# A fused hybrid encoder step: first norms run ahead, first operands built without GpSimd, and x re-read over tiles that are read early

## The chip, the cores and the metric

The kernel runs on 1 core of one Trainium2 chip. The metric is the device time of one execution in microseconds (us), of which the median over several runs is compared. The core has five engines with a queue of instructions each: TensorE (PE; its weight loads are PEld), VectorE (DVE), ScalarE (ACT), GpSimd (POOL) and SyncE (SP), which here issues the DMAs.

## The reference, cut to what matters

```python
mod = silu(c) @ w_ada + b_ada              # shift, scale, gate for 3 sub-layers
h = rms_norm(x) * gain * (1 + sc1) + sh1   # sub-layer 1
gate, up = split(h @ w_up);  x = x + 0.5 * g1 * ((silu(gate) * up) @ w_down)
h = adaRMS(x);  projections, stick-breaking heads, retention heads;  x = x + g2 * mixed
h = adaRMS(x);  x = x + 0.5 * g3 * swiglu(h)  # sub-layer 3
```

There are 1024 tokens of a new stream and 64 of a running one (1088 columns), D_MODEL = 1024 (8 tiles of 128 rows), D_FF = 2816 (22 tiles). All is fp32. The kernel splits each fp32 operand into a high and a low part, and makes each product of two operands from three matmuls (high x high, low x high, high x low).

## The kernel before, in words

x lies transposed in eight tiles `A0` to `A7` of 128 x 1088. The kernel runs in this order: a head (norm of sub-layer 1, its shift and scale, its operands), the up product of sub-layer 1 for f = 0 to 21, the down product of sub-layer 1, the mixed heads, sub-layer 3. The change touches the head, and by its placing of tiles the seam between the up and the down product.

**The head.** x comes in three chunks of columns (384, 384, 320). For each, ACT squares the eight tiles (L262), POOL and DVE add the squares up (`sq`, L265), PE folds them over partitions (`st`, L272), DVE and POOL make the row factors (`ra` L214, `rx` L215), PE spreads them over the partitions (`rb`, L221), and DVE multiplies x in place (L667 before, L669 after). The shift and scale of each of the eight tiles kt, in the order 0, 4, 1, 5, 2, 6, 3, 7, take the weight tiles `au`, PE sums (`pa`, L675), a copy to SBUF on DVE (`pe`), PE's turn of it (`pm`, L686), and on DVE `mod` and `scale_a`. `pa` and `pm` have one PSUM bank each.

**The first operands.** The up product is done with seven products instead of eight (a Strassen-Winograd scheme, `ORDER` p1, p6, p5, p7, p2, p4, p3). For each k = 0 to 3, from `A[k]` and `A[k+4]`, ACT makes four modulated blocks b11, b12, b21, b22 (L407, in tiles `hn`, eight buffers in all), DVE and POOL make four differences t1 = b12 - b11, t2 = b22 - t1, t3 = b22 - b12, t4 = b21 - t2 (L412), and each of seven of these is split: ACT casts the high part (L225), DVE or POOL subtracts it (L226). The matmuls of p1, p6 and p5 for f = 0 are taken k by k as the operands come; they read b11, t2 and t1. In the rows, `xt23` is the split of t2 for k = 3, `hn0t23` that difference before its split, and `xb` and `hn0b` the same for the b blocks.

**The weights.** `wr` are raw weight tiles (four buffers), `wh` and `wl` their high (ACT, L81) and low parts (POOL, L86), seven buffers each. `wr1s` and some `wr1a` are sums of raw tiles that DVE makes (L466).

**The seam.** The operands of the up product lie in 28 tiles, among them the eight A tiles. After f = 21 the kernel loads x into the A tiles again (L772 before, L779 after), for which the last product that reads a tile must be done. The down product then adds PE's result into A (`resid`, L243, on DVE). Beside it DVE makes the next modulation from the rows `wa` and the silu of c, `csil` (L743 before, L750 after), one step after the sixth of each eight results; here DVE goes in the order in which the program is written. PE writes its results to eight PSUM banks in turn. The SP queue starts each DMA in its place in the queue, after all that the DMA has to wait for.

Of the kernel before, what the change touches and what calls it, by code (L numbers as in the profile page):

```python
# [24 lines left out]
CHUNKS = [(0, 384), (384, 384), (768, 320)]  # L25
# [13 lines left out]
def drain(gen):  # L39
    for _ in gen:  # L40
        pass
# [74 lines left out]
def tile_hybrid_step(ctx: ExitStack, tc: tile.TileContext, I, O):  # L116
    nc = tc.nc
# [39 lines left out]
    def pt(tag, name):  # L157
        return psum.tile([P, 512], F32, tag=tag, name=name, bufs=BANKS[tag])
# [65 lines left out]
    def split_h(src, hi, lo, eng):  # L224
        nc.scalar.copy(hi, src)  # L225
        eng.tensor_tensor(lo, src, hi.bitcast(F32), op=ALU.subtract)  # L226
# [127 lines left out]
    SETS = ("b11", "t1", "t2", "b21", "t3", "t4", "b22")  # L354
# [27 lines left out]
    def x_whole(pool):  # L382

        tags = [(hpool, f"{t}{k}") for k in range(KT) for t in "HL"] + [(pool, f"xe{i + 2}") for i in range(4)]
        for k in range(4):
            for i, name in enumerate(SETS):
                if i < 5:
                    p, tag = tags[5 * k + i]
                else:
                    p, tag = xpool, f"A{k + 4 * (i - 5)}"  # L390
                yield k, name, p, tag

    def x_parts(parts, pool, n, k, s, whole):

        w = 2 * BL if whole else BL
        b = {}

        def new(name):
            return pool.tile([P, w], F32, tag="hn", name=f"hn{n}{name}{k}{s}", bufs=8)

        for name, kt, lo, x in parts:
            h = b[name] = new(name)
            if not whole:
                nc.vector.tensor_tensor(h, A[kt][:, lo:lo + w], x, op=ALU.mult)
            src = A[kt][:, lo:lo + w] if whole else h
            for s0, sw, bt in ([(lo, w, 0)] if lo + w <= NPR else [(lo, NPR - lo, 0), (NPR, NSM, 1)]):
                nc.scalar.activation(h[:, s0 - lo:s0 - lo + sw], src[:, s0 - lo:s0 - lo + sw], AF.Identity,  # L407
                                     bias=mod[:, 3 * n, bt, kt:kt + 1], scale=scale_a[:, n, bt, kt:kt + 1])

        def less(name, x, y, eng):  # L410
            t = b[name] = new(name)
            eng.tensor_tensor(t, b[x], b[y], op=ALU.subtract)  # L412

        less("t1", "b12", "b11", nc.vector)
        less("t2", "b22", "t1", nc.vector)
        less("t3", "b22", "b12", nc.gpsimd)
        less("t4", "b21", "t2", nc.vector)
        return b

    def x_build_whole(k, n, pool, places):  # L420

        h = 2 * BL
        b = x_parts((("b11", k, 0, None), ("b12", k, h, None), ("b21", k + 4, 0, None), ("b22", k + 4, h, None)),
                    pool, n, k, "", True)
        for i, name in enumerate(("b11", "t2", "t1", "t3", "b21", "t4", "b22")):
            p, tag = places[k, name]
            t = p.tile([P, NTOK], F32R, tag=tag, name=f"x{name}{k}", bufs=1)
            split_h(b[name], t[:, :h], t[:, h:], nc.gpsimd if i in (1, 3, 5) else nc.vector)
            for part in range(2):
                for s in range(2):  # L430
                    X[name, part, k, s] = t[:, (2 * part + s) * BL:(2 * part + s + 1) * BL]
# [190 lines left out]

    xe = tc.alloc_tile_pool(name="xe1", bufs=1, reuse_waits="tile")
    places = {(k, name): (p, tag) for k, name, p, tag in x_whole(xe)}
    up = Up(1, I["wup1"], hd[:FFT])
    with tc.tile_pool(name="st", bufs=1, reuse_waits="tile") as pool:
        pools["tmp"] = pool
        cT = pool.tile([P, KT, 2], F32, name="cT")
        bada = pool.tile([P, 9, KT], F32, name="bada")
        for t, nm in ((cT, "cT"), (bada, "bada"), (gains, "gains")):  # L630
            nc.sync.dma_start(t, I[nm])
        adau, adae = {}, {}
        pairs = [0, 4, 1, 5, 2, 6, 3, 7]

        def ada_load(kt):
            for s in (1, 0):
                t = adau[s, kt] = pool.tile([P, D], F32, tag="au", name=f"au{s}_{kt}", bufs=4)
                nc.sync.dma_start(t, I["wada01"][s * KT + kt])

        for c, (c0, w) in enumerate(CHUNKS):  # L640
            for k in range(KT):
                nc.sync.dma_start(A[k][:, c0:c0 + w], I["x"][k][:, c0:c0 + w])
        for kt in pairs[:2]:
            ada_load(kt)
        weights = up.prep(0)
        next(weights)
        next(weights)
        cS = pool.tile([P, KT, 32], F32, name="cS")
        nc.gpsimd.memset(cS, 0.0)
        nc.scalar.activation(cS[:, :, 0:2], cT, AF.Silu)  # L650
        sel = pool.tile([P, 2], F32, name="sel")
        nc.vector.tensor_reduce(sel, ident.rearrange("p (j x) -> p x j", x=32)[:, 0:2, :],
                                axis=mybir.AxisListType.X, op=ALU.add)
        for kt in pairs[2:]:
            ada_load(kt)
        nc.sync.dma_start(qkg, I["qkg"])

        ns = [Norm(0, c, pool, ("pj", "z", "wt")[c]) for c in range(3)]

        def norm_first(c):  # L660

            c0, w = CHUNKS[c]
            ns[c].fold()
            ns[c].factors()
            ns[c].rows(("pj", "z", "wt")[c])
            for kt in pairs:
                nc.vector.tensor_tensor(A[kt][:, c0:c0 + w], A[kt][:, c0:c0 + w], ns[c].rb[:, :w], op=ALU.mult)  # L667

        def ada_sums(kt):  # L669

            pa = pt("ms", f"pa{kt}")
            for s in (1, 0):
                for k in range(KT):
                    j = k % 4
                    nc.tensor.matmul(pa[32 * j:32 * j + 32, s * P:(s + 1) * P], cS[:, k, :],  # L675
                                     adau[s, kt][:, k * P:(k + 1) * P], start=k < 4, stop=k >= 4)
            pe = adae[kt] = pool.tile([P, 256], F32, tag="pe", name=f"pe{kt}", bufs=2)
            with tc.high_priority(offset=500):
                nc.vector.tensor_copy(pe, pa[:, :256])

        def ada_turn(kt):

            pe = adae.pop(kt)
            pm = pt("av", f"pm{kt}")
            for s in (1, 0):
                nc.tensor.matmul(pm[:, 2 * s:2 * s + 2], pe[:, s * P:(s + 1) * P], sel, start=True, stop=True)  # L686
            with tc.high_priority(offset=500):
                for s in (1, 0):
                    nc.vector.tensor_scalar(mod[:, s, :, kt], pm[:, 2 * s:2 * s + 2], bada[:, s, kt:kt + 1], None,
                                            op0=ALU.add)  # L690
                nc.vector.tensor_scalar(scale_a[:, 0, :, kt], mod[:, 1, :, kt], 1.0, gains[:, 0, kt:kt + 1],
                                        op0=ALU.add, op1=ALU.mult)

        with tc.manual_schedule(engines={mybir.EngineType.PE}):
            for c in range(3):
                for d in range(KT):
                    ns[c].square(d)
                norm_first(c)
            ada_sums(pairs[0])
            ada_sums(pairs[1])  # L700
            drain(weights)
            for k in range(4):
                for kt in pairs[2 * k:2 * k + 2]:
                    ada_turn(kt)
                if k < 3:
                    for kt in pairs[2 * k + 2:2 * k + 4]:
                        ada_sums(kt)
                if k > 0:
                    for p in ORDER[:3]:
                        for s in range(2):  # L710
                            up.product(0, p, s, [k - 1])
                x_build_whole(k, 0, pool, places)
            for p in ORDER[:3]:
                for s in range(2):
                    up.product(0, p, s, [3])
# [610 lines left out]
    for i, blk in enumerate((0, 2, 1, 3)):  # L1326
        c0 = blk * BL
# [64 lines left out]
    for g in range(FFT // 2):  # L1392
        for _, final in down.steps(g):
            if final is not None:
                c, d = final
                c0, w = CHUNKS[c]
# [100 lines left out]
```

## Time and profile before

| | us |
|---|---|
| median of 3 runs | 2334.13 |
| lowest and highest | 2331.98 to 2338.8 |
| profiled execution, device time | 2335.12 |
| its span | 2333.3 |
| PE busy | 2192.5 (94%) |
| DVE busy | 1510.1 (65%) |
| POOL busy | 1078.1 (46%) |
| ACT busy | 833.6 (36%) |

The span runs from the first to the last instruction of the profiled execution. Its device time is 1.8 us longer, and stands 1.0 us above the median. Busy shares are means over the whole span.

### The profile page before, as it was taken

How to read it: one execution, taken by the hardware profiler on the slowest of the kernel's cores; microseconds unless marked ns; L12 is line 12 of the kernel's file. 1: busy time of each engine (PE TensorE's matmuls, PEld its weight loads, DVE VectorE, ACT ScalarE, POOL GpSimd, SP SyncE). 2: the span in 40 equal slices, each digit the busy share in tenths (PEclk: the TensorE clock that was granted, in tenths of full speed). 3: DMA queues.
4: the chain of work that ended last, by engine and by line, in shares of the span. 5: the costliest groups of instructions: out<-in, count | busy, mean ns of one | idle time of the engine just before them, and what ended most of it. 6: DMA issues, size and time to landing. Idle time of an engine off the chain costs nothing. (4 is left out here: it accounts for less than half of the span.)

```text
span 2333.3 us, 40156 instructions
## 1 busy us (share of the span) xinstructions
PE 2192.5 (94%) x15188; PEld 2147.3 (92%) x15188; DVE 1510.1 (65%) x2886; ACT 833.6 (36%) x1724; POOL 1078.1 (46%) x1020
## 2 busy tenths in 40 slices
PE   5799999998999988888989999967999999999999
PEld 4799999998999988888889998967999999999999
DVE  5867677654777777787784455477555555556666
ACT  4533232332122336665663333156322223322221
POOL 4644444453444556444343444255444444544442
PEclk9799999999999989999999999977999999999999
DMA  6233333336434311010101112122222222353323
GB/s 234 89 124 119 120 121 128 116 115 203 133 118 136 119 54 62 32 41 24 39 26 62 40 36 103 49 86 74 93 80 89 91 93 74 108 179 86 102 81 101
DMA packets 116609, 220.35 MB, mean 94 GB/s; under 512 B 14528, under 2 KB 55488, under 8 KB 116416
## 3 DMA queue, kind: packets, MB, share of 16 engines
q1 hardware_dynamic: 116416, 217.79, 28.4%
q8 instruction: 120, 1.97, 0.4%
q14 instruction: 73, 0.60, 0.1%
HBM read 174.88 MB, written 42.86 MB: 93 GB/s over the span
## 5 line engine op out<-in xcount | busy, mean ns | idle before, releaser
L243 DVE SCALAR_TENSOR_TENSOR A<-dn,mod,A 128x384 f32<-128x384 f32 (+1 forms) x704 | 329.8, 496 | 149.5 <-PE dn L199 148.9
L197 PE MATMUL dn<-hs,wh 128*128 128x384 f32 (+1 forms) x1056 | 348.8, 330 | 7.9 <-DVE A L243 7.9
L198 PE MATMUL dn<-hs,wl 128*128 128x384 f32 (+1 forms) x1056 | 348.0, 330 | 0.0
L199 PE MATMUL dn<-hl,wh 128*128 128x384 f32 (+1 forms) x1056 | 348.0, 330 | 0.0
L86 POOL TENSOR_TENSOR wl<-wr,wh 128x512 fp32r<-128x512 f32 x162 | 220.6, 1368 | 136.2 <-ACT wh L81 131.3
L226 POOL TENSOR_TENSOR hl<-hr,hs 128x384 fp32r<-128x384 f32 x132 | 132.7, 1022 | 239.1 <-ACT hs L225 237.1
L197 PE MATMUL pj<-Hh,wh 128*128 128x384 f32 (+1 forms) x672 | 237.0, 353 | 2.3 <-DVE A L243 2.3
L199 PE MATMUL pj<-Lh,wh 128*128 128x384 f32 (+1 forms) x672 | 224.5, 334 | 0.0
L198 PE MATMUL pj<-Hh,wl 128*128 128x384 f32 (+1 forms) x672 | 223.1, 332 | 0.0
L197 PEld LDWEIGHTS dn<-hs,wh 128*128 128x128 f32 x1056 | 199.1, 189 | 8.3 <-DVE A L243 8.2
L198 PEld LDWEIGHTS dn<-hs,wl 128*128 128x128 f32 x1056 | 199.1, 189 | 0.0
L199 PEld LDWEIGHTS dn<-hl,wh 128*128 128x128 f32 x1056 | 199.0, 188 | 0.0
L518 DVE TENSOR_TENSOR u<-p,p 128x272 f32<-128x272 f32 x176 | 77.3, 440 | 167.7 <-PE p L199 167.7
L225 ACT CAST hs<-hr 128x384 fp32r<-128x384 f32 x132 | 65.3, 496 | 328.3 <-PE dn L198 154.9
L197 PE MATMUL p<-xt,wh1s 128*128 128x272 f32 x528 | 154.5, 293 | 2.5 <-DVE u L518 2.5
L198 PE MATMUL p<-xt,wl1s 128*128 128x272 f32 x528 | 154.2, 292 | 0.0
L199 PE MATMUL p<-xt,wh1s 128*128 128x272 f32 x528 | 153.9, 292 | 0.2
L81 ACT CAST wh<-wr 128x512 fp32r<-128x512 f32 x162 | 98.1, 619 | 148.7 <-PE wo L199 50.1
L86 POOL TENSOR_TENSOR wl1a<-wr1a,wh1a 128x512 fp32r<-128x512 f32 x66 | 93.3, 1415 | 94.6 <-ACT wh1a L81 88.2
L86 POOL TENSOR_TENSOR wl2a<-wr2a,wh2a 128x512 fp32r<-128x512 f32 x66 | 87.5, 1327 | 102.0 <-ACT wh2a L81 101.2
L197 PEld LDWEIGHTS pj<-Hh,wh 128*128 128x128 f32 x672 | 129.0, 192 | 5.3 <-issue 3.3
L198 PEld LDWEIGHTS pj<-Hh,wl 128*128 128x128 f32 x672 | 129.1, 192 | 0.3
(326 smaller groups left out, 6723.5 us busy)
## 6 DMA issues: line engine op xcount, KB each, us to landing
wa<-in_wada SPq DMA_DIRECT2D x56, 512.0 KB, 3.6
hd<-hh SPq DMA_DIRECT2D x44, 544.0 KB, 2.8
wr1a<-in_wup SPq DMA_DIRECT2D x88, 256.0 KB, 2.8
wr<-in_wdn SPq DMA_DIRECT2D x88, 256.0 KB, 2.9
wr2a<-in_wup SPq DMA_DIRECT2D x88, 256.0 KB, 2.8
hr<-hd SPq DMA_DIRECT2D x88, 192.0 KB, 2.7
wr<-in_win SPq DMA_DIRECT2D x56, 256.0 KB, 2.7
au<-in_wada SPq DMA_DIRECT2D x16, 512.0 KB, 4.7
```

The lines of the kernel that those rows point to most:

```text
L81: self.nc.scalar.copy(h, raw)
L86: self.nc.gpsimd.tensor_tensor(l, raw, h.bitcast(F32), op=ALU.subtract)
L197: nc.tensor.matmul(ps[:, :w], wh, xh, start=first, stop=False, skip_group_check=read_between)
L198: nc.tensor.matmul(ps[:, :w], wl, xh, start=False, stop=False, skip_group_check=read_between)
L199: nc.tensor.matmul(ps[:, :w], wh, xl, start=False, stop=last, skip_group_check=read_between)
L225: nc.scalar.copy(hi, src)
L226: eng.tensor_tensor(lo, src, hi.bitcast(F32), op=ALU.subtract)
L243: nc.vector.scalar_tensor_tensor(A[d][:, s0:s0 + sw], ps[:, s0 - c0:s0 - c0 + sw], mod[:, s, b, d:d + 1], A[d][:, s0:s0 + sw], op0=ALU.mul ...
L518: nc.vector.tensor_tensor(new(name), ps[:, :BL], v[y, s], op=ALU.add)
```

## The change

All row sums and factors of the three chunks are now written ahead of the products with them (the products of a chunk come after the next chunk's factors, those of the last chunk with the pair of tiles that needs them). The sums of a pair of tiles and their turns are written together, a pair earlier. t3 and the low parts that POOL had (16 instructions of 128 x 544 in all) are made on DVE. And in the placing of the 28 operand tiles the A tiles get t2 and t1, where they had t4 and b22.

```diff
@@ -383,7 +383,7 @@
         for k in range(4):
-            for i, name in enumerate(SETS):
+            for i, name in enumerate(("b11", "b21", "t3", "t4", "b22", "t2", "t1")):
                 if i < 5:
                     p, tag = tags[5 * k + i]
                 else:
@@ -413,7 +413,7 @@
-        less("t3", "b22", "b12", nc.gpsimd)
+        less("t3", "b22", "b12", nc.vector if whole else nc.gpsimd)
@@ -422,10 +422,10 @@
-        for i, name in enumerate(("b11", "t2", "t1", "t3", "b21", "t4", "b22")):
+        for name in ("b11", "t2", "t1", "t3", "b21", "t4", "b22"):
...
-            split_h(b[name], t[:, :h], t[:, h:], nc.gpsimd if i in (1, 3, 5) else nc.vector)
+            split_h(b[name], t[:, :h], t[:, h:], nc.vector)
@@ -658,12 +658,14 @@
         def norm_first(c):
-
-            c0, w = CHUNKS[c]
             ns[c].fold()
             ns[c].factors()
             ns[c].rows(("pj", "z", "wt")[c])
-            for kt in pairs:
+
+        def scaled(c, kts):
+
+            c0, w = CHUNKS[c]
+            for kt in kts:
                 nc.vector.tensor_tensor(A[kt][:, c0:c0 + w], A[kt][:, c0:c0 + w], ns[c].rb[:, :w], op=ALU.mult)
@@ -696,15 +698,20 @@
                 norm_first(c)
-            ada_sums(pairs[0])
-            ada_sums(pairs[1])
+                if c > 0:
+                    scaled(c - 1, pairs)
+            for kt in pairs[:2]:
+                ada_sums(kt)
+            for kt in pairs[:2]:
+                ada_turn(kt)
             drain(weights)
             for k in range(4):
-                for kt in pairs[2 * k:2 * k + 2]:
-                    ada_turn(kt)
+                scaled(2, pairs[2 * k:2 * k + 2])
                 if k < 3:
                     for kt in pairs[2 * k + 2:2 * k + 4]:
                         ada_sums(kt)
+                    for kt in pairs[2 * k + 2:2 * k + 4]:
+                        ada_turn(kt)
```

A scheduler orders what is written, except on PE in the head and on DVE beside the down product. Three places show what it made of it.

The first place is DVE in the head, from the factors of the first chunk on: `A0` to `A7` are the products with the row factors `rb0_0`, `sq0_1_4` is the sum of squares of the second chunk and `ra` the start of its factors. Before:

```order
L214 TENSOR_SCALAR ra_268<-st0_0_260 128x3
L265 TENSOR_TENSOR sq0_1_4_294<-sq0_1_4_294,sq0_1_5_296 128x384
L667 TENSOR_TENSOR A0_75<-A0_75,rb0_0_271 128x384
L667 TENSOR_TENSOR A4_79<-A4_79,rb0_0_271 128x384
L667 TENSOR_TENSOR A1_76<-A1_76,rb0_0_271 128x384
L667 TENSOR_TENSOR A5_80<-A5_80,rb0_0_271 128x384
L667 TENSOR_TENSOR A2_77<-A2_77,rb0_0_271 128x384
L667 TENSOR_TENSOR A6_81<-A6_81,rb0_0_271 128x384
L667 TENSOR_TENSOR A3_78<-A3_78,rb0_0_271 128x384
L667 TENSOR_TENSOR A7_82<-A7_82,rb0_0_271 128x384
L265 TENSOR_TENSOR sq0_1_4_294<-sq0_1_4_294,sq0_1_6_299 128x384
```

After it the same stretch reads:

```order
L214 TENSOR_SCALAR ra_268<-st0_0_260 128x3
L265 TENSOR_TENSOR sq0_1_4_286<-sq0_1_4_286,sq0_1_5_288 128x384
L669 TENSOR_TENSOR A0_75<-A0_75,rb0_0_271 128x384
L265 TENSOR_TENSOR sq0_1_4_286<-sq0_1_4_286,sq0_1_6_291 128x384
L669 TENSOR_TENSOR A4_79<-A4_79,rb0_0_271 128x384
L265 TENSOR_TENSOR sq0_1_4_286<-sq0_1_4_286,sq0_1_7_294 128x384
L669 TENSOR_TENSOR A1_76<-A1_76,rb0_0_271 128x384
L214 TENSOR_SCALAR ra_305<-st0_1_297 128x3
L669 TENSOR_TENSOR A5_80<-A5_80,rb0_0_271 128x384
```

The adds of the second chunk moved between the products of the first, and its factors ahead of five of them; the third chunk's stand in the same way among the second's products.

The second place is DVE at the last of the four blocks, k = 3, down to `u2`, the first step behind the head that reads PE's products. Before:

```order
L412 TENSOR_TENSOR hn0t13_794<-hn0b123_786,hn0b113_784 128x544
L412 TENSOR_TENSOR hn0t23_796<-hn0b223_791,hn0t13_794 128x544
L226 TENSOR_TENSOR xb113_802<-hn0b113_784,xb113_802 128x544
L412 TENSOR_TENSOR hn0t43_800<-hn0b213_789,hn0t23_796 128x544
L226 TENSOR_TENSOR xt13_808<-hn0t13_794,xt13_808 128x544
L226 TENSOR_TENSOR xb213_814<-hn0b213_789,xb213_814 128x544
L226 TENSOR_TENSOR xb223_820<-hn0b223_791,xb223_820 128x544
L466 TENSOR_TENSOR wr1a11_1_897<-wr1a11_1_897,wr1a21_1_895 128x512
L518 TENSOR_TENSOR u2_10_0_850<-p6_10_0_592,p1_10_0_846 128x272
```

And after:

```order
L412 TENSOR_TENSOR hn0t23_796<-hn0b223_791,hn0t13_794 128x544
L412 TENSOR_TENSOR hn0t33_798<-hn0b223_791,hn0b123_786 128x544
L412 TENSOR_TENSOR hn0t43_800<-hn0b213_789,hn0t23_796 128x544
L226 TENSOR_TENSOR xb113_802<-hn0b113_784,xb113_802 128x544
L226 TENSOR_TENSOR xt23_805<-hn0t23_796,xt23_805 128x544
L226 TENSOR_TENSOR xt13_808<-hn0t13_794,xt13_808 128x544
L226 TENSOR_TENSOR xt33_811<-hn0t33_798,xt33_811 128x544
L226 TENSOR_TENSOR xb213_814<-hn0b213_789,xb213_814 128x544
L226 TENSOR_TENSOR xt43_817<-hn0t43_800,xt43_817 128x544
L226 TENSOR_TENSOR xb223_820<-hn0b223_791,xb223_820 128x544
L466 TENSOR_TENSOR wr1a11_1_897<-wr1a11_1_897,wr1a21_1_895 128x512
L518 TENSOR_TENSOR u2_10_0_850<-p6_10_0_600,p1_10_0_846 128x272
```

t3 and the splits of t2, t3 and t4 joined DVE's row: eleven instructions of 128 x 544 for a k (with the first, t1, above the piece), where it had seven.

The third place is the SP queue at the seam: `wr2` to `wr5` are raw weights of the down product, `A1_0` to `A1_7` the tiles into which x is loaded, `hd21` takes the last result of the up product to memory. Before, x stood behind five weight tiles, and the rows of the modulation right behind x:

```order
L76 DMA wr2_0_6497<-in_wdn1 128x512
L76 DMA wr2_1_6499<-in_wdn1 128x512
L76 DMA wr3_0_6582<-in_wdn1 128x512
L76 DMA wr3_1_6584<-in_wdn1 128x512
L76 DMA wr4_0_6766<-in_wdn1 128x512
L772 DMA A1_0_6450<-in_x 128x384
L772 DMA A1_1_6451<-in_x 128x384
```

After, the 24 loads of x follow `wr2_0`, and this stands between the last of them and the modulation's rows:

```order
L779 DMA A1_7_6457<-in_x 128x320
L76 DMA wr2_1_6499<-in_wdn1 128x512
L76 DMA wr3_0_6582<-in_wdn1 128x512
L76 DMA wr3_1_6584<-in_wdn1 128x512
L76 DMA wr4_0_6766<-in_wdn1 128x512
L76 DMA wr4_1_6768<-in_wdn1 128x512
L542 DMA hd21_112<-hh121_6390 128x1088
L76 DMA wr5_0_6847<-in_wdn1 128x512
L733 DMA csil7_6485<-in_cond 128x1024 x2
L741 DMA wa7_0_6557<-in_wada 128x1024
```

The loads of x moved ahead of four weight tiles and of `hd21`, and seven transfers moved in between x and `csil`, `wa`. On ACT two casts of these weights now stand before and behind the last silu of the up product, `wh2_1` ahead of it. Beyond the head and the seam the rows of all engines are those of before.

## Rows read from the trace of the kernel before

**Rows 1.** The page's slices: PE busy in tenths, 40 slices of 58.3 us.

```profile
PE   5799999998999988888989999967999999999999
```

**Rows 2.** Windows: busy us (instructions) of PE, PEld, DVE, ACT, POOL; PE clock, DMA share, GB/s.

```profile
60.00:70.00 10.00, 7.61 (x90) 6.65 (x90) 9.67 (x14) 5.59 (x11) 8.30 (x5) 0.66 0.02 6
```

**Rows 3.** Waits of PE from 100 to 800 us: total, times, longest.

```profile
PE dn L197 <- DVE A L243: 7.9, 1, 7.9
```

**Rows 4.** Timeline of DVE in the head: start, duration, instruction [idle before, releaser].

```profile
17.18 3.81 DVE L667 TENSOR_TENSOR A<-A,rb 128x384 f32<-128x384 f32 x8 [2.46 <-PE rb L221]
20.90 2.50 DVE L265 TENSOR_TENSOR sq<-sq,sq 128x384 f32<-128x384 f32 x4
25.38 0.16 DVE L214 TENSOR_SCALAR ra<-st 128x3 f32<-128x3 f32 x1 [1.98 <-PE st L272]
...
28.42 3.80 DVE L667 TENSOR_TENSOR A<-A,rb 128x384 f32<-128x384 f32 x8 [2.46 <-PE rb L221]
32.14 0.21 DVE L214 TENSOR_SCALAR ra<-st 128x2 f32<-128x2 f32 x2
...
42.14 0.23 DVE L691 TENSOR_SCALAR scale_a<-mod,gains 128x2 f32<-128x2 f32 x1
```

**Rows 5.** Timeline of DVE: t1 of k = 0, 2, 3, a step alone, steps beside POOL.

```profile
44.11 0.71 DVE L412 TENSOR_TENSOR hn0t<-hn0b,hn0b 128x544 f32<-128x544 f32 x1
...
71.27 0.71 DVE L412 TENSOR_TENSOR hn0t<-hn0b,hn0b 128x544 f32<-128x544 f32 x1
...
74.70 0.71 DVE L412 TENSOR_TENSOR hn0t<-hn0b,hn0t 128x544 f32<-128x544 f32 x1
75.34 1.87 DVE L226 TENSOR_TENSOR xt<-hn0t,xt 128x544 fp32r<-128x544 f32 x1
77.13 3.64 DVE L226 TENSOR_TENSOR xb<-hn0b,xb 128x544 fp32r<-128x544 f32 x2
80.70 1.87 DVE L412 TENSOR_TENSOR hn0t<-hn0b,hn0b 128x544 f32<-128x544 f32 x1
...
91.82 0.78 DVE L518 TENSOR_TENSOR u<-p,p 128x272 f32<-128x272 f32 x2
```

**Rows 6.** Timeline of POOL in the same stretch.

```profile
74.90 5.29 POOL L226 TENSOR_TENSOR xt<-hn0t,xt 128x544 fp32r<-128x544 f32 x3 [1.41 <-ACT xt L225]
```

**Rows 7.** Timeline of ACT: the two parts of b22 for k = 0.

```profile
45.16 1.11 ACT L407 ACTIVATE hn0b<-A,mod,scale_a 128x480 f32<-128x480 f32 x2
```

**Rows 8.** Timeline of PE: the first matmul behind the head's products.

```profile
92.31 0.60 PE L197 MATMUL p<-xt,wh1s 128*128 128x272 f32 x1 [2.48 <-DVE u L518]
```

**Rows 9.** Timeline of the SP queue at the seam.

```profile
544.16 4.22 SPq L772 DMA_DIRECT2D A<-in_x  x9
...
550.18 8.47 SPq L772 DMA_DIRECT2D A<-in_x  x15
...
559.64 0.96 SPq L734 DMA_DIRECT2D wa<-in_wada  x2
```

**Rows 10.** Timeline of DVE at the seam.

```profile
532.46 0.44 DVE L518 TENSOR_TENSOR u<-p,p 128x272 f32<-128x272 f32 x1 [1.06 <-PE p L199]
...
568.31 1.23 DVE L743 SCALAR_TENSOR_TENSOR junk<-wa,csil 128x1024 bf16<-128x1024 f32 x1 [13.89 <-DMA wa<-in_wada]
```

**Rows 11.** Timeline of ACT at the seam: a cast behind p5, the silu behind p3.

```profile
535.45 0.62 ACT L81 CAST wh<-wr 128x512 fp32r<-128x512 f32 x1 [2.40 <-PE p L199]
...
548.02 0.43 ACT L539 ACTIVATE c<-c 128x272 f32<-128x272 f32 x1
```

**Rows 12.** Windows at the seam, columns as in rows 2.

```profile
565.00:570.00 5.00, 0.00 (x0) 0.00 (x0) 1.69 (x4) 2.11 (x2) 0.00 (x0) 0.66 0.85 335
```

**Rows 13.** Timeline of PE behind its wait at the seam.

```profile
570.13 0.69 PE L197 MATMUL dn<-hs,wh 128*128 128x384 f32 x1 [7.88 <-DVE A L243]
...
573.47 0.34 PE L198 MATMUL dn<-hs,wl 128*128 128x384 f32 x1
573.65 0.34 PE L199 MATMUL dn<-hl,wh 128*128 128x384 f32 x1
```

## The prediction

> **What bounds the kernel now.** I read the slices first: PE is at 9 tenths in most of them, and the first two stand at 5 and 7 [rows 1]. What is cheap to lose there is all that the head holds back from PE, so I looked for the places where PE waits. From 100 to 800 us there is one, 7.9 us long, on the DVE step that adds a result into A [rows 3]. The change touches the head and this seam; the rest of the program keeps its order on every engine, PE-bound, and will shift as a block. The reader is to see two different limits.
>
> In the head DVE is the limit: in the window from 60 to 70 us it is busy 9.67 of 10 us, and POOL 8.30 [rows 2]. It is busy, but much of it is waiting inside the instruction. A step of 128 x 544 alone is followed by the next after 0.64 us (74.70 to 75.34). The three steps from 75.34 run beside three POOL steps and take until 80.77, 5.43 us [rows 5, 6]. Alone they would take 1.9, so each POOL step costs DVE (5.43 - 1.9) / 3 = 1.18 us. PE goes on without breaks from 92.31, after DVE's first `u` at 91.82 [rows 5, 8].
>
> At the seam the wait's last link reads as DVE, but DVE itself stands 13.89 us for `wa` [rows 10]. It takes its steps in written order, so the results behind `wa` stay in their banks, and PE runs out of banks at 570.13 - 7.88 = 562.25. The row of `wa` is issued at 559.64, behind the 24 loads of x that begin at 544.16 [rows 9], and is in at 568.31. PE starts 1.82 us after that [rows 10, 13]. So the SP queue and the DMA engines, at 335 GB/s in that window [rows 12], set the end of this wait; the loaded x is not what comes last.
>
> **The change, part by part.**
>
> *Norms ahead of products.* The last add of the second chunk's squares on DVE stood third of four from 20.90 that took 2.50, so it ended near 22.8 [rows 4]. Now it stands behind two products and one add from 17.18, at 0.48 each (3.81 / 8), and ends near 19.1. From that add to `ra` are 2.55 us (22.8 to 25.38), from `ra` to the first product 3.04 (25.38 to 28.42) [rows 4]. I carry both over: `ra` of chunk 2 at 21.7, its products from 24.7, the third chunk's last add four products and two adds later and done by 26.7, its `ra` at 29.25 instead of 32.14. The sums and turns of the first pair hang on this, so `scale_a` at 42.14 [rows 4] comes 2.9 us earlier, near 39.3. The five products behind each `ra` cost nothing more, since they fill part of the 3.04 us in which PE and POOL make the factors; without that cover they cost 5 x 0.48 = 2.4. Ahead of the first t1 now stand two weight sums and three products, some 3.1 us, so t1 of k = 0 moves only from 44.11 [rows 5] to about 42.4: **-1.7**.
>
> *POOL's 16 steps on DVE.* Four a k: each adds 0.64 and takes away 1.18 of blocking. The bound on the good side is 16 x (1.18 - 0.64) = 8.6 us. The bound on the bad side is that nothing comes back and each costs 1.18 + 0.64 = 1.82 beside weight splits: 29 us more. I take the value cycle by cycle, since other waits appear once POOL is out. The blocks and differences have eight buffers, as many as one k uses, so b22 of the next k can be written only when the last split of this k is done. ACT needs 1.1 us for it [rows 7], then 0.55 for the cast behind it; DVE has one t1 (0.64) to do meanwhile. A clean k is then 11 x 0.64 + 1.0 = 8.0 us.
> - k = 0 and 1 took 71.27 - 44.11 = 27.2 us [rows 5]. After: 2 x 8.0, six weight splits of POOL, which stay (6 x 1.0, less than 1.18 as some fall into idle time), seven copies and turns with their two-engine round trips (about 5.0), one weight sum 0.6: 27.6, **+0.4**.
> - k = 2 took 80.70 - 71.27 = 9.4, after 8.0: **-1.4**.
> - k = 3 up to `u` took 91.82 - 80.70 = 11.1. After: 8.0 + one weight split 1.2 + one weight sum 0.6 = 9.8: **-1.3**.
>
> Together the head gives -4.0, and PE goes on near 88.3 instead of 92.31. Its clock there is no part of the sum: it starts from a half-idle stretch before and after. The Trainium skill, page "Perfetto Trace Analysis", section "Optimizing Scalar/DVE Operations", speaks against this part: when VectorE is saturated it says that handing work to ScalarE, or even GpSimd, may make sense, and this does the reverse; the same sentence adds that the two share a read port, so that the hand-over might not help. By its first half the 16 steps would lengthen a saturated engine by 16 x 0.64 = 10 us; by its second half and the 1.18 above they shorten it, and the sum goes by the row.
>
> *Turns pair by pair.* PE turns a pair before the products of the k before instead of behind them. This moves DVE's small steps earlier, inside the 27.6 above. What would be late is the first copy of the next sums, behind PE's products of 18 matmuls; the round trip has that in it. The load of `qkg` and two bias rows move behind the `au` loads; sub-layer 2 uses them hundreds of us later, so 21 passes of the up product hide them, and without that cover they would cost one landing.
>
> *The seam.* The loads of x wait for the last reader of each tile. A0 to A3 now hold t2, read by p6, whose second half was done by 532.46; A4 to A7 hold t1, read by p5, done by 535.45 [rows 10, 11]. Before they began at 544.16 [rows 9]. x is 128 x 1088 x 8 x 4 bytes = 4.46 MB. Five loads (0.98 MB) fit before 535.45; the other 3.47 MB need 10.4 us at 335 GB/s and end near 546. The weight tile `wr2_1` comes next and lands near 548.4. ACT's cast of it (0.62) now stands ahead of the last silu, which was at 548.02 [rows 11] and moves to 549. Behind that silu wait the last product with it on DVE, `hd21` on SP, and behind `hd21` one weight tile, `csil` and `wa`. So `wa` is issued near 553 instead of 559.64. From 550.5 on, two weight tiles, `hd21`, `csil` and `wa` are still to move: 0.52 + 0.56 + 1.05 + 0.52 = 2.65 MB, 7.9 us. `wa` is in near 558.4, ten us earlier. PE does not wait if it is in by 562.25 - 1.82 = 560.4. So the 7.88 goes, and its follow-up too: the granted clock of 565 to 570 is 0.66 [rows 12], PE has stood, and the ten matmuls from 570.13 take 3.34 us, at the lower of the two levels (1.2 of 2.4 GHz), against 10 x 0.18 at 573.47 [rows 13]: 1.5 us. **-9.4**. What is next in line is the tenth weight tile's slot, which needs POOL's split of `wr2_1`; that is about 550.5 and inside the sum.
>
> Sum: -4.0 - 9.4 = -13.4 us, from the profiled 2335.12 to 2321.7. The median of the runs is 1.0 us below the profiled time, so 2320.7; I say 2321.
>
> **The rivals.**
>
> *The head gives nothing (17%).* The two-engine round trips and the eight buffers leave DVE idle as long as POOL blocked it. For it: +0.4 in k = 0 and 1 already shows how little is left. Against: k = 2 and 3 have no turns in them. Time: 2334 - 9.4 = 2325.
>
> *The head gives all (10%).* The waits overlap, and the whole 8.6 and a head start of 2.9 come through: 2334 - 9.4 - 11.5 = 2313.
>
> *The wait at the seam stays (12%).* Seven more transfers, 2.1 MB, now stand between x and `wa`, and a late `wr2_1` holds ACT, DVE and `hd21` in turn. Each us by which `wr2_1` lands after 550.4 (548.4 plus the spare 2.0) is a us of PE's wait. With `wa` at 566 the wait is still 5.6 and the clock falls too: 2334 - 4.0 - 2.3 = 2328. For it: PE's row already blamed the wrong engine once. Against: x starts 11.7 us earlier (532.46 against 544.16), and 2.1 MB take 6.4.
>
> *DVE becomes the bound (6%), slower.* If POOL's steps are not what stretches DVE's, the 16 come on top at 1.23 us, the middle of 0.64 and 1.82: 19.7 us, against the start's 1.7 and the seam's 9.4: 2334 + 8.6 = 2343. It decides from (1.7 + 9.4) / 16 = 0.7 us net for a moved step. For it: DVE is at 9.67 of 10 us [rows 2]. Against: the step at 74.70 took 0.64 while POOL stood, and 1.87 right after beside it [rows 5, 6].
>
> **How the numbers follow.** The forecast has 55%, with its own range 2317 to 2326 (the head between -1 and -7, the seam between -7.5 and -9.4). The range 2313 to 2328 leaves out the slower case, half of the seam's rival and little of the one with all gains. A run of this kernel tells 0.3% (7.0 us) from no change. Faster by more than that: the forecast, the full gain, nearly all of the head's rival and a third of the seam's, 0.85. Within it: 0.09. Slower: 0.06.
>
> **What would show it.** In the head: steps of 128 x 544 on DVE at 0.64 to 0.72 except beside weight splits, `scale_a` of the first pair near 39.5, PE without breaks from about 88. At the seam: loads of x from about 532, `wa` issued near 553, no wait of PE on A, and no lower clock behind it. Wrong would be: DVE idle by many us for ACT's blocks or PE's turns in the head; a silu or `hd21` long behind 551; or a PE wait that moved to another step.

## The result and the profile after

| | before | after |
|---|---|---|
| median of the runs | 2334.13 us (2329.82 to 2338.8) | 2316.76 us (2316.09 to 2324.65) |
| profiled execution | 2335.12 us, span 2333.3 | 2316.76 us, span 2314.7 |
| ratio after / before | | 0.9938, 95% interval 0.992 to 0.9957 |

The change takes 17.4 us off the median and 18.6 us off the profiled span, against 13 forecast. The ratio over all runs says less, 14.5 us (10 to 18.7): three of the five runs after lie at 2316 to 2317 us, the other two at 2321.7 and 2324.7. Three rows of PE divide the 18.6, since each has the same matmul in both traces: the first behind `u` in the head [rows 8], the first behind the wait at the seam [rows 13], and, in the projection that follows, the first `pj` that waits for A (called the `pj` row below). After:

```profile
84.42 0.39 PE L197 MATMUL p<-xt,wh1s 128*128 128x272 f32 x1 [0.90 <-DVE u L518]
...
556.77 0.44 PE L197 MATMUL dn<-hs,wh 128*128 128x384 f32 x1 [3.40 <-DVE A L243]
...
825.56 0.41 PE L197 MATMUL pj<-Hh,wh 128*128 128x384 f32 x1 [1.71 <-DVE A L243]
```

The `pj` row of the kernel before, in the same view:

```profile
838.83 0.41 PE L197 MATMUL pj<-Hh,wh 128*128 128x384 f32 x1 [2.34 <-DVE A L243]
```

- **Head**: PE goes on at 84.42 instead of 92.31, -7.9 us. Forecast -4.0.
- **From there to the `pj` row**: 825.56 - 84.42 = 741.1 instead of 838.83 - 92.31 = 746.5, -5.4 us. Forecast -9.4 (the seam). PE runs dry at 556.77 - 3.40 = 553.37 where it was 562.25, so some 1.0 of the 5.4 came just behind the head, and 4.4 at the seam.
- **Rest**: 2314.7 - 825.56 = 1489.1 instead of 2333.3 - 838.83 = 1494.5, -5.3 us. Forecast nothing.

**The head.** DVE's timeline after, start, duration, instruction, answering to [rows 4, 5]:

```profile
22.15 0.16 DVE L214 TENSOR_SCALAR ra<-st 128x3 f32<-128x3 f32 x1 [1.93 <-PE st L272]
28.86 0.22 DVE L214 TENSOR_SCALAR ra<-st 128x2 f32<-128x2 f32 x2 [1.59 <-PE st L272]
37.92 0.22 DVE L693 TENSOR_SCALAR scale_a<-mod,gains 128x2 f32<-128x2 f32 x1
41.19 0.42 DVE L681 COPY pe<-pa 128x256 f32<-128x256 f32 x1 [1.46 <-PE pa L677]
42.33 1.07 DVE L412 TENSOR_TENSOR hn0t<-hn0b,hn0b 128x544 f32<-128x544 f32 x1
...
67.90 0.71 DVE L412 TENSOR_TENSOR hn0t<-hn0b,hn0b 128x544 f32<-128x544 f32 x1
71.08 1.98 DVE L226 TENSOR_TENSOR xt<-hn0t,xt 128x544 fp32r<-128x544 f32 x3
74.89 0.71 DVE L412 TENSOR_TENSOR hn0t<-hn0b,hn0b 128x544 f32<-128x544 f32 x1
83.93 0.78 DVE L518 TENSOR_TENSOR u<-p,p 128x272 f32<-128x272 f32 x2
```

The reader is to compare the distances of the three `t1` rows (42.33, 67.90, 74.89) and of `u` with those in [rows 5]: k = 0 and 1 take 25.6 instead of 27.2, k = 2 takes 7.0 instead of 9.4, k = 3 up to `u` takes 9.0 instead of 11.1, and the start is 1.8 earlier. Three splits in a row take 1.98 here; beside POOL's three, three splits took 5.43 before. The window that answers to [rows 2], same columns:

```profile
60.00:70.00 10.00, 6.00 (x31) 4.95 (x32) 10.00 (x19) 7.41 (x15) 4.82 (x3) 0.66 0.50 157
```

DVE does 19 instructions here instead of 14 in the same 10 us, eleven of 128 x 544 instead of five, while POOL has three weight splits left. DVE was called busy before and is called busy now; only the count tells the two apart.

**The seam.** The waits of PE from 80 to 800 us, which answer to [rows 3]:

```profile
PE dn L197 <- DVE A L243: 3.4, 1, 3.4
PE p L197 <- DVE u L518: 0.9, 1, 0.9
```

So the wait at the seam has shrunk, not gone. The SP queue after, answering to [rows 9] (times of before are those of after plus 8.9 here):

```profile
523.23 12.98 SPq L779 DMA_DIRECT2D A<-in_x  x24
536.33 7.74 SPq L76 DMA_DIRECT2D wr<-in_wdn  x5
544.16 0.38 SPq L542 DMA_DIRECT2D hd<-hh  x1
545.21 0.33 SPq L76 DMA_DIRECT2D wr<-in_wdn  x1
545.62 1.15 SPq L733 DMA_DIRECT2D csil<-in_cond  x2
546.83 1.57 SPq L741 DMA_DIRECT2D wa<-in_wada  x2
```

The loads of x start at 523.23, which is 532.1 on the clock of before, as forecast (532). But `wa` is issued at 555.7 on that clock, not 553. ACT and DVE show what held it:

```profile
541.73 0.62 ACT L81 CAST wh<-wr 128x512 fp32r<-128x512 f32 x1 [3.75 <-PE dn L199]
542.26 0.43 ACT L539 ACTIVATE c<-c 128x272 f32<-128x272 f32 x1
```

```profile
542.72 1.30 DVE L521 TENSOR_TENSOR hh<-c,c 128x272 f32<-128x272 f32 x1 [2.46 <-ACT c L539]
554.95 1.23 DVE L750 SCALAR_TENSOR_TENSOR junk<-wa,csil 128x1024 bf16<-128x1024 f32 x1 [8.31 <-DMA wa<-in_wada]
```

ACT stands 3.75 us ahead of the cast of `wr2_1`. The row names a matmul as what ended this wait; in a second profile of the same kernel, whose seam is like this one, it names the load:

```profile
542.45 0.62 ACT L81 CAST wh<-wr 128x512 fp32r<-128x512 f32 x1 [3.61 <-DMA wr<-in_wdn]
```

The last silu follows the cast at 542.26, 551.1 on the clock of before (forecast 549); then come `hh`, `hd21`, one weight tile, `csil` and `wa`, each behind the one before. Meanwhile the DMA engines run out of work, as the windows show (columns as in [rows 2]):

```profile
525.00:530.00 5.00, 5.00 (x42) 5.00 (x42) 1.32 (x3) 1.02 (x2) 1.86 (x2) 1.00 0.89 269
...
535.00:540.00 5.00, 5.00 (x39) 5.00 (x38) 2.70 (x7) 0.43 (x1) 0.00 (x0) 1.00 1.02 342
540.00:545.00 5.00, 5.00 (x30) 5.00 (x29) 2.54 (x5) 1.46 (x3) 2.57 (x2) 1.00 0.43 142
545.00:550.00 5.00, 5.00 (x30) 5.00 (x29) 1.64 (x4) 1.03 (x2) 2.16 (x3) 1.00 0.97 296
550.00:555.00 5.00, 3.37 (x20) 3.05 (x18) 0.05 (x1) 2.12 (x2) 0.00 (x0) 1.00 0.94 356
```

From 540 to 545 they moved 142 GB/s between stretches of 342 and 296: the queue stood at the fifth weight tile (the row of five from 536.33 ends at 544.07). `wa` is in at 554.95, 563.8 on the clock of before, against 558.4 forecast and 560.4 allowed: 3.4 us too late.

`wr2_1` itself came late with x, which stands ahead of it. From 525 to 530 the DMA engines moved 269 GB/s, not 335, and the view of tile A from 523 to 545 shows how long each takes to land:

```profile
DMA to landing us min/median/max: 3.5/4.1/5.2
```

The last load of x was issued at 535.9, so it landed between 539.4 and 541.1, which is 548.3 to 550.0 on the clock of before; the forecast had x in near 546. What held the rate down was not traced.

### The profile page after: what moved, and what is told of

It reads as the page before. It is cut to its first block, busy times and chain, and to the rows that moved or that the text cites. A ratio compares the mean times of both kernels' runs of the same rounds, so it can differ in the third digit from the quotient of the medians.

```text
span 2314.7 us, 40167 instructions
## 1 busy us (share of the span) xinstructions
PE 2184.9 (94%) x15188; PEld 2140.0 (92%) x15188; DVE 1505.9 (65%) x2902; ACT 832.8 (36%) x1724; POOL 1051.6 (45%) x1004
```

## The experiments

The ratios are those of the times to the times of the kernel before on the same chip. The runs come from several chips, on which the kernel before had medians of 2337.58 us (head only, places only, both kernels with `wa` later), 2336.31 (POOL kept, POOL's steps alone, weight splits, `wr` early) and 2337.49 (both edits). The table divides every profiled span at the same rows as above. All kernels compute the whole reference.

| kernel | ratio, interval | PE behind `u` | from there to the `pj` row | wait at the seam | wait at `pj` | rest |
|---|---|---|---|---|---|---|
| before | | 92.31 | 746.5 | 7.9 | 2.34 | 1494.5 |
| changed | 0.9938 (0.992 to 0.9957) | 84.42 | 741.1 | 3.4 | 1.71 | 1489.1 |
| head only | 0.9947 (0.9929 to 0.9965) | 84.16 | 745.9 | 7.1 | 1.74 | 1489.4 |
| places only | 0.9969 (0.9957 to 0.9981) | 91.98 | 742.0 | 4.8 | 2.38 | 1494.8 |
| POOL kept | 0.9964 (0.9949 to 0.9979) | 88.81 | 742.7 | 2.9 | 2.44 | 1494.2 |
| POOL's steps alone | 0.9954 (0.9937 to 0.9971) | 85.41 | 746.7 | 8.3 | 1.94 | 1488.7 |
| weight splits on DVE | 0.9964 (0.9947 to 0.9982) | 90.66 | 739.7 | 2.0 | 2.26 | 1497.9 |
| changed, `wa` later | 0.9899 (0.9884 to 0.9915) | 84.01 | 737.0 | none | 2.44 | 1491.8 |
| before, `wa` later | 0.9943 (0.9929 to 0.9957) | 92.72 | 735.4 | none | 2.49 | 1494.1 |
| changed, `wr` early | 0.9902 (0.9885 to 0.9918) | 83.68 | 736.0 | none | 1.82 | 1488.9 |
| changed, both | 0.9904 (0.9889 to 0.9919) | 83.10 | 735.9 | none | 1.74 | 1486.4 |

**The two halves apart.** *Head only* is the changed kernel with the old order of x's places:

```diff
-            for i, name in enumerate(("b11", "b21", "t3", "t4", "b22", "t2", "t1")):
+            for i, name in enumerate(SETS):
```

> The change without its new placing of the operand tiles: the head alone. If the head and the seam are two separate gains, PE goes on behind the head at 84.4 us as with the whole change (7.9 earlier than before), the seam keeps its 7.9 us wait of PE, and the time is 8 to 10 us under before, near 2325. If the later 5 us (PE's clock between 835 and 850 us of the trace of before) is chance of one execution, it shows in this profile or not, whatever the seam does. If instead the placing has a hand in the head (A tiles written over by t2 and t1 early), PE goes on at another time than 84.4.

Measured: 2323.19 us, 14.4 under before where 8 to 10 were expected; a rest that is 5.1 us shorter in its profile is part of that. PE goes on at 84.16, and the seam's wait is 7.1, near the 7.9 of before. *Places only* is the kernel before with the new order (the same line the other way round):

> The kernel before with the new placing alone. Two separate gains: PE goes on behind the head at 92.3 as before, its wait at the seam is about 3.4 us instead of 7.9, and the time is some 4.5 us under before, near 2330. The rival, that the wait at the seam only shrank since the head shifted everything, gives 7.9 us here and no gain.

Measured: 2329.83 us, 7.8 under before (4.5 expected). The head ends at 91.98, as before; the wait is 4.8, not 3.4. Up to the `pj` row the head alone gains 8.8 us and the places alone 4.9, together 13.7 against 13.3 for the whole change. So the halves are separate: the head comes from the order of norms, the turns and the moved steps, and the shorter wait from the places of x. How short is less sure, as one program (weight splits on DVE, below) waited 2.0 us in one profile and 4.9 in another.

**Within the head: the 16 steps or the order.** *POOL kept* is the changed kernel with those steps on POOL; *POOL's steps alone* makes the opposite edit in the kernel before.

```diff
-        less("t3", "b22", "b12", nc.vector if whole else nc.gpsimd)
+        less("t3", "b22", "b12", nc.gpsimd)
...
-            split_h(b[name], t[:, :h], t[:, h:], nc.vector)
+            split_h(b[name], t[:, :h], t[:, h:], nc.gpsimd if i in (1, 3, 5) else nc.vector)
```

> The changed kernel with the 16 steps (t3, and the low parts of t2, t3 and t4) back on GpSimd; norms ahead, turns pair by pair and the new placing stay. If POOL's steps cost DVE by blocking it, the order alone gives little: PE goes on behind the head at 89 to 91 us (the start comes 1.8 earlier), and DVE's steps of 128 x 544 beside POOL take 1.8 again. If the order of norms and turns made the gain, PE goes on near 85.

> The kernel before with the 16 steps on DVE and nothing else. If POOL's blocking is the cost, PE goes on behind the head at 86 to 87 us (6 us of the 7.9); if the order of norms and turns is what made room, DVE with eleven steps a k and the old turns ends at 91 or later, up to 16 x 0.64 = 10 us later than before if nothing comes back.

Measured: 2326.34 and 2323.85 us. With POOL's steps back PE goes on at 88.81 (89 to 91 expected), so they are worth 4.4 us in the changed kernel; alone in the kernel before they bring 85.41 (86 to 87 expected), 6.9 us. The rest of the head gives 3.5 alone and 1.0 on top. The two gains overlap: together they are 7.9, not 10.4. DVE in the kernel with POOL kept, where the steps stretch again:

```profile
71.23 1.86 DVE L412 TENSOR_TENSOR hn0t<-hn0b,hn0t 128x544 f32<-128x544 f32 x1
73.02 1.88 DVE L226 TENSOR_TENSOR xt<-hn0t,xt 128x544 fp32r<-128x544 f32 x1
```

and POOL's steps in the same kernel, beside them:

```profile
70.69 5.42 POOL L226 TENSOR_TENSOR xt<-hn0t,xt 128x544 fp32r<-128x544 f32 x3
```

A step of this shape is 1.86 there and 0.71 at 67.90 and 74.89 in the changed kernel. The Trainium skill, page "SBUF — State Buffer", section "Who interferes with whom", says that a VectorE instruction with two inputs in SBUF contends with a GpSimd instruction that reads SBUF; for VectorE's modes that take two ports it adds that whoever issues first holds the shared pair for the whole instruction and the other is blocked in full. The trace agrees on the contention: a DVE step beside a POOL step is followed by the next after 1.79 us (71.23 to 73.02), against 0.64 alone, and POOL's three steps take 5.42, 1.81 each. So DVE goes at POOL's pace there, one step for one; which of the two was blocked in each pair the rows do not tell.

**The same cure for the weight splits.** POOL still splits the weights in the head. Seven of them were moved to DVE:

```diff
+            self.w[f, name] = (h, wu.low(r, h, f"{self.n}{name}_{f}", nc.vector if f == 0 and self.n == 1 else None))
```

> The changed kernel with the seven low parts of the first weights on DVE too, so that no POOL step reads beside DVE in the head but for the last one. The same theory: each costs DVE 0.62 itself and gives back what it blocked, which the trace of the changed kernel puts at 3.9 us over six of them; PE goes on within 1 us of 84.4, no gain left. If each weight split blocks a full 1.18 us, it gives 3 us: near 81.5.

Measured: 2329.2 us, and PE goes on at 90.66, 6.2 us later than in the changed kernel, which neither theory had. PE's timeline, around the last pair of the modulation:

```profile
51.34 1.01 PE L688 MATMUL pm<-sel,pe 128*128 128x2 f32 x4 [0.88 <-DVE mod L691]
71.38 0.59 PE L197 MATMUL p<-xt,wh1s 128*128 128x272 f32 x1 [15.41 <-DVE A L669]
72.35 1.94 PE L677 MATMUL pa<-au,cS 128*32 128x128 f32 x32
```

PE stood 15.41 us, and the sums of the last pair, which stand behind these products in PE's written order, came at 72.35; in the changed kernel they came at 57.19. DVE, which had been ahead until 70, then waited for them. The row's last link is a product of the last pair with its factors, and on DVE these products had moved behind the splits:

```profile
70.43 0.89 DVE L669 TENSOR_TENSOR A<-A,rb 128x320 f32<-128x320 f32 x2
```

In the changed kernel the last of them starts by 42. Why that matmul waits for them is not shown. So this run does not price the weight splits; it shows that what one engine's order gains is lost where another engine's written order hangs on it.

**The seam: is `wa` alone late?** The first products with `wa` were put three steps later in DVE's written order, once in the changed kernel and once in the kernel before:

```diff
-                    drain(down.steps(g, lambda c: ada.upto((3 * g + c + 1) / (3 * (FFT // 2 - 1)))))
+                    drain(down.steps(g, lambda c: ada.upto(max(0, 3 * g + c - 2) / (3 * (FFT // 2 - 2)))))
```

> The changed kernel with the modulation rows beside the down product of sub-layer 1 begun three steps later (one pass of two f), the same work in all. If DVE stands for wa, and x itself is in on time, the 3.4 us wait at the seam goes to zero, the lower clock behind it too (another 1.5), and the time is 4 to 5 us under the changed kernel. If x is what is late, the wait stays at 3 us or more, now on the loads of x.

> The kernel before with the modulation rows begun three steps later, and the old placing. If wa alone is late at the seam, the 7.9 us wait goes without any new placing, and the time is 8 to 10 us under before. If x comes too late over tiles that p4 and p3 read last, a wait of 3 us or more stays, on the loads of x, and the new placing is needed.

Measured: 2311.73 and 2323.22 us (5.0 under the changed kernel, as expected, and 14.4 under before, where 8 to 10 were), and PE waits nowhere on A from 80 to 800 us in either. Up to the `pj` row they gain 4.5 and 10.7 us. In the second, x is still loaded from 543.09, as in [rows 9], with the old places. So it was `wa` that was late, never x; x mattered only by standing ahead of it.

**The seam: what made `wa` late.** Three of the raw weight tiles that follow x in the queue were asked for ahead of it, in the changed kernel; they now stand among the loads of x:

```diff
+        wu.load(U_DN1 + 3)
         a_tiles(F32, "A1_")
```

> The changed kernel with the weight tiles of the third and fourth f asked for ahead of x, so that they stand among the loads of x and not behind them. If the chain of wr2_1, ACT's cast, the last silu, hd21, csil and wa is what left 3.4 us of PE's wait, the silu comes 2 us earlier, wa is in by 552 and the wait is 1 us or less, without a lower clock behind it: 3 to 5 us under the changed kernel. If only the bytes ahead of wa count, which are the same, the wait stays at 3 us.

Measured: 2310.59 us, 6.2 under the changed kernel (3 to 5 expected). SP's queue in this kernel, from the last loads of x on:

```profile
531.23 6.74 SPq L780 DMA_DIRECT2D A<-in_x  x13
538.13 0.80 SPq L76 DMA_DIRECT2D wr<-in_wdn  x2
540.17 0.33 SPq L542 DMA_DIRECT2D hd<-hh  x1
540.59 0.38 SPq L76 DMA_DIRECT2D wr<-in_wdn  x1
541.06 1.80 SPq L733 DMA_DIRECT2D csil<-in_cond  x2
542.96 1.20 SPq L741 DMA_DIRECT2D wa<-in_wada  x2
```

and its window from 540:

```profile
540.00:545.00 5.00, 5.00 (x30) 5.00 (x29) 3.57 (x7) 0.00 (x0) 0.00 (x0) 1.00 0.98 353
```

`wa` is issued 3.9 us earlier than in the changed kernel (542.96 against 546.83), the hole in the DMA's work is gone (353 GB/s against 142), and PE does not wait. The bytes ahead of `wa` are the same, so the rival in which they alone count is out. From `u` to the `pj` row it takes 736.0 us against 746.5: 10.5 us. If 1.0 of it came behind the head, as in the changed kernel, the other 9.5 are the seam's 9.4 as forecast. The step that failed was thus the landing of `wr2_1` behind x, not the worth of the wait.

Both edits together take the same wait only once:

> The changed kernel with both edits that took the wait at the seam away: the last three raw down weights of the previous stage are loaded ahead of x, and the first products with wa stand three steps later in VectorE's handwritten order. Theory (either edit takes the same wait, 3.4 us and the 1 to 2 us of low clock behind it): the two together give no more than one alone, 2310 to 2312, the same as the kernel with the early raw weights. Rival: the later products also take load off VectorE behind the seam, and the time falls to 2306 or below.

Measured: a median of 2316.44 us (2307.34 to 2318.52), above the 2310 to 2312 expected, ratio 0.9904: no more than either alone. Its profiled execution, 2307.34, is the lowest of its five by 8.5 us, and its mean granted clock is 0.976 against 0.967 to 0.968 in the other four.

**The 5.3 us behind the seam.** Windows of the projection, from 3 to 7 us behind the `pj` row, before:

```profile
842.00:846.00 4.00, 4.00 (x18) 3.97 (x19) 3.04 (x6) 0.26 (x1) 2.29 (x3) 0.50 0.00 0
```

and after:

```profile
829.00:833.00 4.00, 4.00 (x26) 3.81 (x27) 4.00 (x6) 0.71 (x2) 2.85 (x4) 1.00 0.00 0
```

PE is busy all through in both, but does 18 matmuls at a granted clock of 0.50 (1.2 GHz) before, and 26 at 1.00 (2.4 GHz) after. No instruction there was changed. Matched matmul by matmul, the two traces part by 4.6 of the 5.3 us within 12 us of the `pj` row. Was it the change, or the execution? The changed kernel was profiled again:

> The changed kernel with nothing changed, profiled once more. In its first profile TensorE's granted clock stayed at 1.00 where that of the kernel before, and of five of the other kernels, was at 0.50 for about 10 us behind a DVE wait near 835 us (on the clock of before), and some 4 to 5 us of the span went with that. Theory: this stretch comes or does not come in one execution of the same program, so the times of one kernel lie in two groups some 5 us apart, near 2316 and near 2322 to 2325; a profile that has the stretch has a span of about 2319 to 2320. Head and seam are the same as in the first profile (PE behind u at 84.4, a wait of 3.4 at the seam). Rival: the change itself keeps the clock up there; then the stretch stays away in this profile, too, and all times lie near 2316.

Measured: 2318.92 us (2317.46 to 2326.84), ratio 0.9933; the clock stayed up again, with a wait of 1.79 and a rest of 1489.1. PE went on behind `u` at 83.76, and the seam's wait was 3.3. The profile spoke for the rival; the times did not, since they lie at 2317.5 to 2320.2 and at 2325.8 and 2326.8, not all near 2316. Two more profiles of unchanged kernels:

> The kernel before with nothing changed, profiled once more. In its first profile, PE's wait on A ahead of the first pj matmul behind 835 us was 2.34 us long, and 10 us at a granted clock of 0.50 followed; its span was 2333.3. Theory (the stretch comes or does not come in one execution of one program): it may be missing here, with a wait near 1.8 and a span some 5 us shorter, 2328. Rival (a kernel's own timing fixes it): wait 2.3 to 2.5, the stretch there again, span near 2333.

> The kernel with seven weight splits on VectorE, unchanged, profiled once more. Its ten times lie in two groups, 2321 to 2323 and 2328 to 2332; its first profile was of the upper one, with a wait of 2.26 ahead of pj and the 10 us at a clock of 0.50 behind it. Theory (the stretch belongs to the execution): a profile of the lower group has a wait near 1.8 and no such stretch, one of the upper group has both again. Rival (a kernel's own timing fixes it): wait 2.3 and the stretch, whichever group the time falls in.

The kernel before had its low stretch again (wait 2.30, rest 1498.1, span 2336.2). The kernel with the weight splits on DVE, the same program as in the table, came out without it: 2323.82 us, wait 1.89, rest 1487.8 against 1497.9. Its window four us behind `pj` in this profile:

```profile
838.00:842.00 4.00, 4.00 (x25) 3.81 (x25) 4.00 (x7) 1.13 (x3) 2.42 (x3) 1.00 0.00 0
```

So one program shows both. Its two profiles come from two chips; that the stretch belongs to the execution and not to the chip rests on its ten times on the first one, which lie in two groups. Over all 14 profiles the stretch is there where the wait ahead of the `pj` row is 2.26 us or longer (rest 1491.8 to 1498.1), and missing where it is 1.94 or shorter (rest 1486.4 to 1489.4).

The wait is not where the profiles part. An earlier stretch at the lower clock lies around the first `pj` in all of them, and before it ends sooner than after. PE's first `pj`, and its first matmul behind that stretch, before:

```profile
829.76 0.67 PE L197 MATMUL pj<-Hh,wh 128*128 128x384 f32 x1
...
832.78 0.38 PE L198 MATMUL pj<-Hh,wl 128*128 128x384 f32 x1
```

and after:

```profile
816.47 0.67 PE L197 MATMUL pj<-Hh,wh 128*128 128x384 f32 x1
...
821.08 0.34 PE L197 MATMUL pj<-Hh,wh 128*128 128x384 f32 x1
```

The `pj` row comes 9.07 and 9.09 us behind the first `pj` either way (9.06 to 9.09 in all 14). After, PE spends 4.6 of them at the slower pace instead of 3.0, comes to the wait later and waits 0.6 us less. So a shorter wait tells of an earlier stretch that ended later. What places that stretch is open, and so is whether the change makes the shorter wait likelier: the changed kernel had it in both of its profiles, the kernel before in neither.

## Why the prediction was right, and where its terms were not

Faster, and inside the range; the median is 4 us below the forecast of 2321. The two terms that it did sum came to -13.3 (-7.9 and -5.4) against -13.4, but only because one was too small by as much as the other was too large. That sum is luck; the causes in it, POOL's steps and the wait for `wa`, are borne out.

- **Start of the head, -1.7: right** (-1.8), by two errors that cancel. `ra` came at 22.15 and 28.86 (21.7 and 29.25 forecast; 22.8 to 25.38 is 2.58, not 2.55). `scale_a` came at 37.92 (39.3), but from there to t1 took 4.4 us, not 3.1: DVE stood 1.46 us for PE's sum ahead of the copy at 41.19.
- **"A clean k is then 11 x 0.64 + 1.0 = 8.0 us": the 1.0 was wrong.** k = 2 took 6.99, eleven steps of 0.64 and nothing else: DVE did not wait for b22 there. Four times 1.0 is the whole 3.9 by which the head was undersized: 25.6 for 27.6, 7.0 for 8.0, 9.0 for 9.8. The weight splits, turns and weight sum, at 11.6 for k = 0 and 1, came out as forecast in their sum: 25.6 - 2 x 7.0 = 11.6. By the 3.9 us that I later read for six weight splits, forecast at 6.0, the turns took some 2 us more than their 5.0, a term that no row had given. The 1.0 was the price of a wait that the trace of before did not show, on the reading that b22 can be written only when the last split of the k before is done. That trace already spoke against it, as the rows behind this list show.
- **1.18 us for a POOL step: right.** With POOL kept, a step beside POOL costs 1.79 - 0.64 = 1.15. The moved steps run at 0.64, and the kernel with POOL kept loses 4.4 us. The rival in which DVE becomes the bound is out. The one in which the head gives all (11.5) is nearer at 7.9 than the one in which it gives nothing.
- **"`wa` is in near 558.4": wrong, 563.8.** This is the rival of the wait that stays, at smaller size: 3.4 us left where it had 5.6. The chain was named rightly (`wr2_1`, ACT's cast, the last silu, `hd21`, `wa`), but x was timed at 335 GB/s from its first load on, and was in 2 to 4 us later than the 546 forecast, with `wr2_1` right behind it; and the transfers behind `hd21` were timed as if they could be issued while it was waited for. The silu was 2 us late, the issue of `wa` 2.7, and its landing another 2.7. The term was worth 9.4 only with `wr2_1` early, as the kernel with early `wr` shows (9.5), or with `wa` used later.
- **"No lower clock behind it": wrong**, since the wait stayed; the clock in the window from 555 fell to 0.82.
- **The rest "will shift as a block": wrong by 5.3 us**, 4.6 of them for a stretch of lower clock that one program has in one profile and lacks in another. The 18.6 us of the span thus hold 5.3 that no term had.

**When b22 could be written.** In the trace of before, ACT's six steps for the blocks of k = 3 end at 80.50,

```profile
76.91 3.59 ACT L407 ACTIVATE hn0b<-A,mod,scale_a 128x544 f32<-128x544 f32 x6
```

ahead of the end of the last split of k = 2 at 80.77 [rows 5]. After, ACT's last five steps for k = 2 end at 65.98, and the last split of k = 1 only starts at 67.27:

```profile
63.12 2.86 ACT L407 ACTIVATE hn0b<-A,mod,scale_a 128x480 f32<-128x480 f32 x5
```

```profile
67.27 0.71 DVE L226 TENSOR_TENSOR xb<-hn0b,xb 128x544 fp32r<-128x544 f32 x1
```

Of the eight tiles one, b12, is not split at all; that its buffer is the one that comes free early is my reading, not shown.

## What to carry to other kernels

Price a stretched step by the distance to the next one with and without its neighbour, and then add no wait that no row shows; but where a transfer hangs on a chain of several engines, add up each link's issue, since the queue stands still between them. Before loads are moved ahead, look at what stands behind them in the same queue: here one later use of `wa`, or three small tiles asked for ahead of x on top of the new places, were worth 9 to 11 us between the same two rows where the new places alone gave 4.5. A sum that comes out right is to be checked term by term against the same instructions in both traces.

## What the runs showed of the hardware that was not expected

The granted clock of one unchanged program differs between two of its profiles over 10 us at one place: 0.50 in one, 1.00 in the other. It goes with a wait of PE that differs by 0.4 us (2.26 and 1.89), and with 10.1 us of the time behind it (rest 1497.9 and 1487.8). Matched matmul by matmul, 4.6 of the 10.1 come within 12 us of the `pj` row. The others come at further places of the kind, the first of them 121 to 127 us behind the row, where the granted clock is 0.50 and 1.00 and 1.6 more come. The two profiles of the kernel before, too, differ by 3.6 us in their rest, with the stretch in both. A single profile of each kernel is therefore no basis for a difference of 5 us here, however well its rows are read.
